# Local attention in pairs: paired score products, output tiles of their own, and one block-diagonal product for the meta keys

## The chip, the cores and the metric

The kernel runs on one core of a Trainium2 chip. The metric is the device time of one execution in microseconds (us). TensorE (PE in the profile, with PEld for its weight loads) does the matrix products and transposes, VectorE (DVE) and ScalarE (ACT) the elementwise work, GpSimd (POOL) some fills, and SyncE (SP) issues most of the transfers from memory.

## The reference, cut to what matters

Two transformer blocks follow each other. The change lies in the first one, whose sequence is 16 meta tokens and 512 tokens, with width 1024. Half of its mixer is a gated linear attention (GLA, 4 heads); the other half is a local attention with a sink, 8 query heads of 64 in 2 key groups of 4:

```python
qm, qr = q[:, :N_META], q[:, N_META:]
...
s_meta = jnp.einsum('bnqkgd,bjkd->bnkgqj', qb, km).astype(jnp.float32)
s_win = jnp.einsum('bnqkgd,bnjkd->bnkgqj', qb, kw).astype(jnp.float32)
...
p = sink_softmax(jnp.concatenate([s_meta, s_win], axis=-1),
                 sink[None, None, :, :, None, None]).astype(dtype)
orr = (jnp.einsum('bnkgqj,bjkd->bnqkgd', p[..., :N_META], vm)
       + jnp.einsum('bnkgqj,bnjkd->bnqkgd', p[..., N_META:], vw))
```

A block of 128 queries sees the 16 meta keys, the keys of its own block and those of the block before. Both halves, side by side, go through `w_out`; the result is added to the residual, normed, and enters a feed-forward part (`w_ff1`, squared ReLU, `w_ff2`).

## The kernel before, in words

The order of instructions on each engine is decided when the program is built, by a scheduler; the code gives the order of the steps and the pools their buffers. Products that need full precision are made of three: each operand is split into a high part (by ACT, `split`, L117) and a low part (by DVE, L118), and `mm3` issues low x high, high x low and high x high (L124 to L126).

`attention1` works through a list of steps, `PLAN`: q is a tile of the local queries (`w_sq`), r a tile of the GLA output gate (`w_gr`), p and g are two parts of a GLA chunk, s is one block of 128 queries of the local attention, o splits that block's output, t applies the gate. Tiles of q and r alternate between two PSUM banks (role mm of `PS_A`); scores have one bank (sw), transposes two (pt), and the attention output one (po).

One s step, `swa_block`, does for each of 8 heads one score product of 64 rows (L1632) and a masked reduction on DVE out of the score's bank (L1633). For each group of four heads follow the exponentials on ACT (L1637), the sums, and the scaling of p (L1645 on ACT, L1647 on DVE). Then for each group p is transposed (L1657), copied to SBUF (L1659) and multiplied with the values (L1660): one product for the block's own keys, one for the block before, and one of 16 rows with `mA` for the meta keys. The output in po is copied by DVE over the queries of the block (L1663), and split into `uh` and `ul` by the o step.

Behind the attention, `w_out` is computed in 8 tiles of 24 products; `w_out_ps` holds as many of them as mm has banks, made inside `attention1`. The residual is loaded (L251), `w_open` gives the first feed-forward group a ring of buffers for its weights (`w_load`, L483), and the group's products (`w_prod`, L499) compute x, z and w of a Strassen-like scheme with weights that are added, subtracted and split first (L536 to L555).

## Time and profile before

| what | us |
|---|---|
| median of 3 runs | 1934.77 (1934.54 to 1935.26) |
| the profiled execution | 1935.17 |
| its span in the profile | 1933.4 |
| PE busy | 1897.1 |
| DVE busy | 1482.6 |
| ACT busy | 864.4 |

The span runs from the first to the last instruction of the profiled execution, the rest of its time lies around it. Busy times are sums over the span; what a stage is bound by is read from windows and from what each engine waits for.

### The profile page before, as it was taken

The numbers are of one execution on the slowest core, as the hardware profiler recorded it, in microseconds if no ns is written. First come the engines' busy times: TensorE is split into PE (matmuls) and PEld (weight loads), VectorE is DVE, ScalarE is ACT, GpSimd is POOL, SyncE is SP. The second block draws the span as 40 slices with busy tenths as digits, with TensorE's granted clock in tenths as the row PEclk, the third lists the DMA queues.
The fourth block names the chain that finished last, engine by engine and source line by source line (L and its number), as shares of the span: only waits on it lengthen the run. The fifth ranks groups of instructions, "written<-read, shape, count | busy, mean of one in ns | idle before, by whom it ended". The sixth has DMA issues, their size and how long they took to land.

```text
span 1933.4 us, 27555 instructions
## 1 busy us (share of the span) xinstructions
PE 1897.1 (98%) x10808; PEld 1583.7 (82%) x10808; DVE 1482.6 (77%) x2507; ACT 864.4 (45%) x1406; POOL 9.4 (0%) x31
## 2 busy tenths in 40 slices
PE   8999999999999899999999999999999999999997
PEld 5775589898998699999887777777778888999997
DVE  6687599888888989888878646677758778877776
ACT  4334465443445545444455444344442245444444
POOL 0000000000000000000000000000000000000000
PEclk9999999999999999999999999999999999999999
DMA  5220045444534154546342232333348732333231
GB/s 198 67 61 12 28 176 177 141 145 152 162 111 142 57 175 142 183 137 202 109 142 88 87 119 69 104 96 99 99 145 308 270 116 78 118 112 108 89 99 55
DMA packets 74331, 240.46 MB, mean 124 GB/s; under 512 B 8997, under 2 KB 12214, under 8 KB 74202
## 3 DMA queue, kind: packets, MB, share of 16 engines
q1 hardware_dynamic: 57274, 189.75, 31.3%
q10 hardware_dynamic: 16928, 48.96, 8.0%
q8 instruction: 85, 1.39, 0.3%
q14 instruction: 44, 0.36, 0.1%
HBM read 225.74 MB, written 8.41 MB: 121 GB/s over the span
## 4 chain that ended last, share of the span: by engine, by line
PE 86%; DVE 9%; ACT 2%; DMA 2%; issue 1%; SPq 0%; DVEq 0%; ACTq 0%
PE x L499 12%; PE mm L132 10%; PE mm L131 10%; PE mm L130 10%; PE mm L124 6%; PE w L499 6%; PE mm L125 6%; PE mm L126 6%; PE z L499 3%; DVE wl L118 2%; PE po L1660 1%; PE sw L1632 1%; PE po L1186 1%; PE sc L1165 1%; PE sc L1047 1%
## 5 line engine op out<-in xcount | busy, mean ns | idle before, releaser
L117 ACT ACTIVATE wh<-raw 128x1024 fp32r<-128x1024 f32 (+1 forms) x371 | 386.3, 1044 | 430.6 <-PE mm L132 126.2
L118 DVE TENSOR_TENSOR wl<-raw,wh 128x1024 fp32r<-128x1024 f32 (+1 forms) x371 | 445.9, 1206 | 119.5 <-ACT wh L117 118.4
L132 PE MATMUL mm<-hh,wh 128*128 128x512 f32 (+1 forms) x640 | 244.6, 382 | 0.0
L131 PE MATMUL mm<-hl,wh 128*128 128x512 f32 (+1 forms) x640 | 244.0, 381 | 0.2 <-DVE hl L118 0.2
L130 PE MATMUL mm<-hh,wl 128*128 128x512 f32 (+1 forms) x640 | 241.7, 378 | 0.7 <-DVE res L694 0.7
L124 PE MATMUL mm<-uh,wl 128*128 128x512 f32 x560 | 225.8, 404 | 2.2 <-ACT uh L117 1.9
L126 PE MATMUL mm<-uh,wh 128*128 128x512 f32 x560 | 223.2, 399 | 0.0
L125 PE MATMUL mm<-ul,wh 128*128 128x512 f32 x560 | 222.4, 397 | 0.7 <-DVE ul L118 0.7
L131 PEld LDWEIGHTS mm<-hl,wh 128*128 128x128 f32 x640 | 120.2, 188 | 23.3 <-DVE hl L118 0.7
L130 PEld LDWEIGHTS mm<-hh,wl 128*128 128x128 f32 x640 | 120.1, 188 | 22.9 <-DVE res L694 0.9
L132 PEld LDWEIGHTS mm<-hh,wh 128*128 128x128 f32 x640 | 120.3, 188 | 21.6
L124 PEld LDWEIGHTS mm<-uh,wl 128*128 128x128 f32 x560 | 105.5, 189 | 33.5 <-issue 7.4
L126 PEld LDWEIGHTS mm<-uh,wh 128*128 128x128 f32 x560 | 105.4, 188 | 23.7 <-issue 2.3
L125 PEld LDWEIGHTS mm<-ul,wh 128*128 128x128 f32 x560 | 105.7, 189 | 23.3 <-issue 2.3
L499 PE MATMUL x<-uh,wl 128*128 128x256 f32 x416 | 115.2, 277 | 1.3 <-DVE wl L118 1.3
L499 PE MATMUL x<-vh,wl 128*128 128x256 f32 x416 | 116.1, 279 | 0.3 <-DVE wq__6174 L559 0.3
L499 PE MATMUL x<-vl,wh 128*128 128x256 f32 x416 | 115.4, 277 | 0.0
L499 PE MATMUL x<-vh,wh 128*128 128x256 f32 x416 | 115.1, 277 | 0.0
L499 PE MATMUL x<-ul,wh 128*128 128x256 f32 x416 | 115.0, 276 | 0.0
L499 PE MATMUL x<-uh,wh 128*128 128x256 f32 x416 | 114.9, 276 | 0.0
L356 DVE CUSTOM_DVE_ANT_0 adaw<-adaw,cb,c_vecs 128x1024 f32<-128x1024 f32 x72 | 91.4, 1277 | 11.1 <-DMA adaw<-in_w_ada 11.0
L622 DVE SCALAR_TENSOR_TENSOR res<-mm,gt,res 128x512 f32<-128x512 f32 x88 | 65.4, 746 | 23.0 <-PE mm L132 22.7
(970 smaller groups left out, 4222.2 us busy)
## 6 DMA issues: line engine op xcount, KB each, us to landing
adaw<-in_w_ada ACTq DMA_DIRECT2D x72, 512.0 KB
raw<-in_wgw SPq DMA_DIRECT2D x72, 512.0 KB
raw<-in_wdw SPq DMA_DIRECT2D x40, 512.0 KB
raw<-in_w_ffw SPq DMA_DIRECT2D x32, 512.0 KB
raw<-in_w_ffd SPq DMA_DIRECT2D x32, 512.0 KB
raw<-in_wgu SPq DMA_DIRECT2D x24, 512.0 KB
raw<-in_w_g SPq DMA_DIRECT2D x20, 512.0 KB
raw<-in_w_out SPq DMA_DIRECT2D x16, 512.0 KB
```

The costliest lines, as they stand in the source:

```text
L117: nc.scalar.activation(out=h, in_=src, func=AF.Copy)
L118: nc.vector.tensor_tensor(out=l, in0=src, in1=h.bitcast(F32), op=ALU.subtract)
L124: mm(ps, lhsT=wl[:, k], rhs=xh[:, k], start=(k == order[0]), stop=False)
L125: mm(ps, lhsT=wh[:, k], rhs=xl[:, k], start=False, stop=False)
L126: mm(ps, lhsT=wh[:, k], rhs=xh[:, k], start=False, stop=(k == order[-1]))
L130: mm(ps, lhsT=al, rhs=bh, start=(k == 0), stop=False)
L131: mm(ps, lhsT=ah, rhs=bl, start=False, stop=False)
L132: mm(ps, lhsT=ah, rhs=bh, start=False, stop=(k == last))
L356: ins = nc.vector.tensor_tensor_reduce(out=w, in0=w, in1=self.cb, scale=0.5, scalar=self.vec("b_ada_2", 72)[:, i:i + 1], op0=ALU.mult, op1 ...
L499: mm(o, lhsT=l[:, a, k], rhs=r(k), start=(first and a == 0 and k == 0 and j == 0), stop=(k == 3 and j == 2), skip_group_check=True)
L622: V.scalar_tensor_tensor(out=res[:, m], in0=ps, scalar=gt[:, m:m + 1], in1=res[:, m], op0=ALU.mult, op1=ALU.add)
L1047: mm(pk[:, :n], lhsT=k[:, kt, j * P:(j + 1) * P], rhs=q[:, kt, j * P:], start=(kt == 0), stop=(kt == 1))
```

## The change

Scores of the two groups, whose operands lie in rows 0 to 63 and 64 to 127, are computed in pairs into a tile of two PSUM banks, and the softmax of both groups follows behind the four pairs. That takes two banks for the scores; mm keeps one bank (0), and pt has banks 1 and 6 instead of 5 and 6. The transposes and value products of both groups are written part by part, with three buffers for pT. The meta keys' values stand in `vmb`, a block-diagonal 64 x 128 tile that is filled by a memset and two small transfers; the first group's p is transposed into rows 0 to 31 of a bank, the second group's is brought into rows 32 to 63 by products with the identity, and one product of 64 rows adds both groups' meta part to po. Three of four scalings are on ACT instead of two. po is split straight into `oh` and `ol`, tiles with a pool of their own, which is closed behind the w_out loop; the ring's pool is opened there, in the same memory. `w_out_tile` reads `oh` and `ol` first, then the GLA half of `uh` and `ul`, and one tile of w_out is made inside `attention1` instead of two. The steps o are gone.

```diff
-PS_A = dict(mm="01", ga="23", sw="4", pt="56", po="7")
+PS_A = dict(mm="0", ga="23", sw="4", pt="16", po="7")
...
-PLAN = "q0 q1 q3 p0 p1 q2 g0 s0 p2 g1 s2 s1 p3 r3 g2 g3 s3 r0 r2 r1 o0 o1 o2 o3 t01 t23"
...
+PTB = 3
+AO_SHIFT = 64
+RSQ = (0.3752467, -1.251589, 1.876343)
+PLAN = "q0 q1 q3 p0 p1 q2 g0 s0 p2 g1 s2 s1 p3 r3 g2 g3 s3 r0 r2 r1 t01 t23"
...
+        oe = ExitStack()
+        op = oe.enter_context(tc.tile_pool(name="ao", bufs=1, side="right"))
+        self.oh, self.ol = (op.tile([P, 4, T], F32R, name=n) for n in ("oh", "ol"))
+        self.shift(op, AO_SHIFT)
...
-        self.w_open(hp, 3)
...
-            ps = self.w_out_ps[m] if m < len(self.w_out_ps) else self.gemm("w_out", m, uh, ul)
+            ps = self.w_out_ps[m] if m < len(self.w_out_ps) else self.w_out_tile(m)
...
+        oe.close()
+        self.w_open(hpe.enter_context(tc.tile_pool(name="ring", bufs=1)), 3)
...
+        vmb = ap.tile([64, P], F32, name="vmb")
+        nc.gpsimd.memset(vmb, 0.0)
+        for g in range(2):
+            nc.sync.dma_start(out=vmb[32 * g:32 * g + NMETA, 64 * g:64 * g + 64], in_=mA[:, 384 + 64 * g:448 + 64 * g])
...
-        self.psum(**PS_A)
+        self.psum(pairs=True, **PS_A)
...
-        self.w_out_ps = [self.gemm("w_out", m, uh, ul, order=(4, 5, 6, 7, 0, 1, 2, 3)) for m in range(self.bufs["mm"])]
+        self.w_out_ps = [self.w_out_tile(m) for m in range(self.bufs["mm"])]
...
+    def w_out_tile(self, m):
+        wh, wl = self.wtile("w_out", m)
+        ps = self.mmps()
+        xs = [(4 + k, self.oh[:, k], self.ol[:, k]) for k in range(4)] + [(k, self.uh[:, k], self.ul[:, k]) for k in range(4)]
+        for j, (k, xh, xl) in enumerate(xs):
+            self.mm3k(ps, wh[:, k], wl[:, k], xh, xl, j)
+        return ps
...
-        pg = []
+        pg = [a2.tile([P, 4, NMETA + 2 * P], F32, name="p", tag="p") for g in range(2)]
+        for a in range(4):
+            pair = self.bank2("sw")
+            for g in range(2):
+                mm(pair[:, g, :W], lhsT=qT[64 * g:64 * g + 64, a, cs], rhs=keys[64 * g:64 * g + 64, :W], start=True, stop=True)
+            for g in range(2):
+                i = g * 4 + a
+                V.tensor_tensor_reduce(out=pg[g][:, a, :W], in0=pair[:, g, :W], in1=mk[:, :W], scale=1.0, scalar=sinks[:, i:i + 1], op0=ALU.add, op1=ALU.max, accum_out=mx[:, i:i + 1])
         for g in range(2):
-            p = a2.tile([P, 4, NMETA + 2 * P], F32, name="p", tag="p")
-            pg.append(p)
-            for a in range(4):
-                i = g * 4 + a
-                ps = self.bank("sw")
-                mm(ps[:, :W], lhsT=qT[64 * g:64 * g + 64, a, cs], rhs=keys[64 * g:64 * g + 64, :W], start=True, stop=True)
-                V.tensor_tensor_reduce(out=p[:, a, :W], in0=ps[:, :W], in1=mk[:, :W], scale=1.0, scalar=sinks[:, i:i + 1], op0=ALU.add, op1=ALU.max, accum_out=mx[:, i:i + 1])
+            p = pg[g]
             gs = slice(4 * g, 4 * g + 4)
             V.tensor_scalar(out=nmx[:, gs], in0=mx[:, gs], scalar1=-1.0, scalar2=None, op0=ALU.mult)
             for i in range(4 * g, 4 * g + 4):
@@ -1641,31 +1662,40 @@
             V.tensor_tensor(out=Z[:, gs], in0=Z[:, gs], in1=es, op=ALU.add)
             V.reciprocal(out=Z[:, gs], in_=Z[:, gs])
             for i in range(4 * g, 4 * g + 4):
-                if i % 2:
+                if i % 4:
                     act(out=p[:, i % 4, :W], in_=p[:, i % 4, :W], func=AF.Copy, scale=Z[:, i:i + 1])
                 else:
                     V.tensor_scalar(out=p[:, i % 4, :W], in0=p[:, i % 4, :W], scalar1=Z[:, i:i + 1], scalar2=None, op0=ALU.mult)
         po = self.bank("po")
-        for g in range(2):
-            parts = [(svt[:, n], P, W - P)]
-            if n > 0:
-                parts.append((svt[:, n - 1], P, NMETA))
-            parts.append((mA[:, 384:512], NMETA, 0))
-            for j, (v, nk, off) in enumerate(parts):
+        def pT(pt, n, func):
+            t = a2.tile([P, T], F32, name="pT", tag="pT", bufs=PTB)
+            func(out=t[:n], in_=pt[:n])
+            return t
+        copy = lambda out, in_: act(out=out, in_=in_, func=AF.Copy)
+        parts = [(svt[:, n], W - P, copy)]
+        if n > 0:
+            parts.append((svt[:, n - 1], NMETA, V.tensor_copy))
+        for j, (v, off, func) in enumerate(parts):
+            ts = []
+            for g in range(2):
                 pt = self.bank("pt")
                 for a in range(4):
-                    tr(pt[:nk, a * P:(a + 1) * P], pg[g][:, a, off:off + nk], ident)
-                pT = a2.tile([P, T], F32, name="pT", tag="pT", bufs=2)
-                (act if j != 1 else lambda out, in_, func: V.tensor_copy(out=out, in_=in_))(out=pT[:nk], in_=pt[:nk], func=AF.Copy)
-                mm(po[64 * g:64 * g + 64], lhsT=v[:, 64 * g:64 * g + 64], rhs=pT[:nk], start=(j == 0), stop=(j == len(parts) - 1))
-        o = qT[:, :, cs]
-        V.tensor_copy(out=o, in_=po.rearrange("p (a t) -> p a t", a=4))
-        return o
-    def swa_out(self, n, o):
-        cs = slice(n * P, (n + 1) * P)
-        self.split(self.uh[:, 4:8, cs], self.ul[:, 4:8, cs], o)
+                    tr(pt[:, a * P:(a + 1) * P], pg[g][:, a, off:off + P], ident)
+                ts.append(pT(pt, P, func))
+            for g in range(2):
+                mm(po[64 * g:64 * g + 64], lhsT=v[:, 64 * g:64 * g + 64], rhs=ts[g], start=(j == 0), stop=False, skip_group_check=True)
+        pt = self.bank("pt")
+        for a in range(4):
+            tr(pt[:32, a * P:(a + 1) * P], pg[0][:, a, 0:32], ident)
+        for a in range(4):
+            mm(pt[32:64, a * P:(a + 1) * P], lhsT=pg[1][:, a, 0:32], rhs=ident, start=True, stop=True)
+        t = pT(pt, 64, copy)
+        mm(po, lhsT=vmb, rhs=t[:64], start=False, stop=True, skip_group_check=True)
+        self.split(self.oh[:, :, cs], self.ol[:, :, cs], po.rearrange("p (a t) -> p a t", a=4))
```

On PE, scores and value products of the last blocks before: sw is a score, ga, po<-S and po<-gv are GLA products, pt transposes.

```order
L1632 MATMUL sw<-kW,qT 128x272
L1660 MATMUL po<-pT,svt 64x512
L1657 MATMUL pt<-ident,p 16x128 x4
L1660 MATMUL po<-pT,svt 64x512
L1576 MATMUL pt<-ident,E 128x128 x2
L126 MATMUL mm<-uh,wh 128x512
L1632 MATMUL sw<-kW,qT 128x272
L1660 MATMUL po<-pT,mA 64x512
L1487 MATMUL ga<-gv,kt 128x256 x2
L1632 MATMUL sw<-kW,qT 128x272
```

The same place now, up to the last pair:

```order
L1688 MATMUL po<-pT,svt 64x512 x2
L1693 MATMUL pt<-ident,p 32x128 x4
L1695 MATMUL pt<-ident,p 32x128 x4
L1595 MATMUL pt<-ident,E 128x128 x2
L1697 MATMUL po<-pT,vmb 128x512
L1506 MATMUL ga<-gv,kt 128x256 x2
L1649 MATMUL sw<-kW,qT 128x272 x2
L1587 MATMUL po<-S_797,E 128x256
L1590 MATMUL po<-gv,A 128x128 x2
L1587 MATMUL po<-S_797,E 128x256
L1590 MATMUL po<-gv,A 128x128 x2
L1649 MATMUL sw<-kW,qT 128x272 x2
```

Two scores stand next to each other where one stood between other work, and the meta part is one product.

On PE behind the last score before; mm<-uh or ul is a w_gr product up to the first transposes of gv, w_out behind them:

```order
L124 MATMUL mm<-uh,wl 128x512
L1660 MATMUL po<-pT,svt 64x512
L1657 MATMUL pt<-ident,p 16x128 x4
L125 MATMUL mm<-ul,wh 128x512
L1660 MATMUL po<-pT,svt 64x512
L126 MATMUL mm<-uh,wh 128x512
L124 MATMUL mm<-uh,wl 128x512
L1660 MATMUL po<-pT,mA 64x512
L125 MATMUL mm<-ul,wh 128x512
L126 MATMUL mm<-uh,wh 128x512
L1606 MATMUL pt<-ident,gv 128x128 x8
L124 MATMUL mm<-uh,wl 128x512 x2
```

And now, from the last pair's transposes to the first products of w_out:

```order
L1685 MATMUL pt<-ident,p 128x128 x8
L1688 MATMUL po<-pT,svt 64x512
L1685 MATMUL pt<-ident,p 128x128 x4
L1688 MATMUL po<-pT,svt 64x512 x2
L1693 MATMUL pt<-ident,p 32x128 x4
L1695 MATMUL pt<-ident,p 32x128 x4
L1625 MATMUL pt<-ident,gv 128x128 x4
L1697 MATMUL po<-pT,vmb 128x512
L1625 MATMUL pt<-ident,gv 128x128 x8
L132 MATMUL mm<-oh,wl 128x512
L133 MATMUL mm<-ol,wh 128x512
L134 MATMUL mm<-oh,wh 128x512
```

No w_gr product stands there any more, and w_out begins with oh.

On SP, the loads around w_out and the start of the feed-forward part before, with the semaphores that each waits for:

```order
L251 DMA res<-in_xT 128x1024
L111 DMA raw<-in_w_out 128x1024 [waits DMAHW0_49,DMAHW7_49,DVE_49,Activation_49]
L483 DMA raw<-in_w_ffw 128x1024 [waits DMAHW1_49]
L483 DMA raw<-in_w_ffw 128x1024 [waits DMAHW2_49]
L111 DMA raw<-in_w_out 128x1024 [waits DMAHW3_49,DVE_49]
L483 DMA raw<-in_w_ffw 128x1024 [waits DMAHW4_49]
L111 DMA raw<-in_w_out 128x1024 [waits DMAHW5_49,DVE_49]
```

And now:

```order
L258 DMA res<-in_xT 128x1024 x2
L113 DMA raw<-in_w_out 128x1024 [waits DMAHW2_49,DVE_49]
L113 DMA raw<-in_w_out 128x1024 [waits DMAHW4_49,DMAHW3_49,DVE_49]
L491 DMA raw<-in_w_ffw 128x1024 [waits DMAHW5_49,DVE_49]
L491 DMA raw<-in_w_ffw 128x1024 [waits DMAHW6_49,DMAHW2_49,DVE_49]
L491 DMA raw<-in_w_ffd 128x1024 [waits DMAHW7_49,DMAHW4_49,DVE_49]
L491 DMA raw<-in_w_ffw 128x1024 [waits DMAHW0_49,PE_49]
L491 DMA raw<-in_w_ffw 128x1024 [waits DMAHW1_49]
L491 DMA raw<-in_w_ffw 128x1024
```

The three loads of the ring (no wait but for their own queue before) now stand behind all of w_out's, and the first of them waits for PE.

## Rows read from the trace of the kernel before

**Rows 1.** The page, parts 1 (busy time) and 4 (the chain that ended last).

```profile
PE 1897.1 (98%) x10808; PEld 1583.7 (82%) x10808; DVE 1482.6 (77%) x2507; ACT 864.4 (45%) x1406; POOL 9.4 (0%) x31
...
PE 86%; DVE 9%; ACT 2%; DMA 2%; issue 1%; SPq 0%; DVEq 0%; ACTq 0%
```

**Rows 2.** Windows: window, its length, busy by engine, PE clock, DMA share, GB/s.

```profile
100.00:215.00 115.00, 114.94 (x541) 75.18 (x540) 88.87 (x288) 51.11 (x151) 1.05 (x2) 1.00 0.12 35
```

**Rows 3.** Timeline of PE: start, duration, line, operands, idle before; scores and neighbours.

```profile
121.73 0.51 PE L1632 MATMUL sw<-kT,qT 64*128 64x144 f32 x2
...
205.98 0.72 PE L1632 MATMUL sw<-kW,qT 64*128 64x272 f32 x2
206.63 1.07 PE L1660 MATMUL po<-pT,mA 16*64 16x512 f32 x2
```

**Rows 4.** Timeline of PE in block 2: two score products of 384 columns.

```profile
1261.01 0.92 PE L1165 MATMUL sc<-g 64*128 64x384 f32 x4
```

**Rows 5.** Timeline of PE: two GLA products; two value products (two records each).

```profile
213.09 0.61 PE L1571 MATMUL po<-gv,A 128*128 128x128 f32 x4
...
216.47 1.93 PE L1660 MATMUL po<-pT,svt 128*64 128x512 f32 x4
```

**Rows 6.** Timeline of PE from the last score to w_out.

```profile
214.51 0.72 PE L1632 MATMUL sw<-kW,qT 64*128 64x272 f32 x2
...
221.00 1.09 PE L1657 MATMUL pt<-ident,p 128*128 128x128 f32 x8
...
230.32 0.73 PE L124 MATMUL mm<-uh,wl 128*128 128x512 f32 x2 [1.93 <-ACT uh L117]
231.73 0.55 PE L125 MATMUL mm<-ul,wh 128*128 128x512 f32 x1 [0.68 <-DVE ul L118]
```

**Rows 7.** Timeline of DVE: the last score's reduction, a w_gr tile's read.

```profile
215.27 0.50 DVE L1633 CUSTOM_DVE_ANT_0 p<-sw,c_mask_w,c_vecs 128x272 f32<-128x272 f32 x1 [2.71 <-PE sw L1632]
...
227.56 0.69 DVE L1425 TENSOR_TENSOR rr<-mm,R 128x512 f32<-128x512 f32 x1
```

**Rows 8.** Timeline of ACT: an exponential and its accumulator's read, two scalings.

```profile
218.13 0.51 ACT L1637 ACTIVATE p<-p,nmx 128x272 f32<-128x272 f32 x1
218.54 0.19 ACT L1637 ACTIVATION_READ_ACCUMULATOR p<-p,nmx 128x1 f32 x1
...
219.52 0.92 ACT L1645 ACTIVATE p<-p,Z 128x272 f32<-128x272 f32 x2
```

**Rows 9.** Windows, columns as in rows 2: the half-clock stretch.

```profile
232.00:235.40 3.40, 3.40 (x11) 2.64 (x11) 3.40 (x6) 1.26 (x2) 0.00 (x0) 0.50 0.00 0
```

**Rows 10.** Timeline of PE: end of w_out, first feed-forward group.

```profile
277.36 0.39 PE L125 MATMUL mm<-ul,wh 128*128 128x512 f32 x1
277.58 0.40 PE L126 MATMUL mm<-uh,wh 128*128 128x512 f32 x1
277.82 0.28 PE L499 MATMUL x<-vh,wl 128*128 128x256 f32 x1
...
288.44 0.39 PE L499 MATMUL x<-uh,wl 128*128 128x256 f32 x1 [1.31 <-DVE wl L118]
```

**Rows 11.** Timeline of SP: issues of 512 KB weight loads.

```profile
240.19 2.77 SPq L483 DMA_DIRECT2D raw<-in_w_ffw  x2
...
394.02 0.33 SPq L425 DMA_DIRECT2D raw<-in_wgu  x1
```

**Rows 12.** Timeline of DVE: feed-forward weight passes; the first read of the load issued at 394.02.

```profile
256.23 2.36 DVE L118 TENSOR_TENSOR wl<-raw,wh 128x1024 fp32r<-128x1024 f32 x2
...
274.93 1.21 DVE L118 TENSOR_TENSOR wl<-raw,wh 128x1024 fp32r<-128x1024 f32 x1
...
398.52 0.29 DVE L427 TENSOR_SCALAR pa<-raw,mods 128x128 f32<-128x128 f32 x1 [1.15 <-DMA raw<-in_wgu]
```

**Rows 13.** Windows of 20 us, columns as in rows 2.

```profile
260.00:280.00 20.00, 20.00 (x99) 16.79 (x98) 19.85 (x29) 12.67 (x18) 0.00 (x0) 1.00 0.26 80
...
300.00:320.00 20.00, 19.76 (x133) 17.75 (x132) 19.48 (x25) 10.99 (x16) 0.00 (x0) 1.00 0.39 125
```

More of the change, by code (lines that the diff above doesn't have):

```diff
@@ L28 @@
 NPRE = 2
-RSQ = (0.3752467, -1.251589, 1.876343)
-PS_A = dict(mm="01", ga="23", sw="4", pt="56", po="7")
+PS_A = dict(mm="0", ga="23", sw="4", pt="16", po="7")
 MM5, AT2, PG1 = "01234", "56", "7"
@@ L1220, in attention1 @@
         wn = self.vec("norm_mix_w")
-        mh = ap.tile([P, KT, NMETA], F32R, name="mh")
-        ml = ap.tile([P, KT, NMETA], F32R, name="ml")
         acc = {}
@@ L1226, in attention1 @@
         x = bp.tile([P, KT, T], F32, name="x")
+        mh = bp.tile([P, KT, NMETA], F32R, name="mh")
+        ml = bp.tile([P, KT, NMETA], F32R, name="ml")
         mt = bp.tile([P, KT, NMETA], F32, name="mt")
@@ L1326, in attention1 @@
         self.dump("kT", kT)
+        vmb = ap.tile([64, P], F32, name="vmb")
+        nc.gpsimd.memset(vmb, 0.0)
+        for g in range(2):
+            nc.sync.dma_start(out=vmb[32 * g:32 * g + NMETA, 64 * g:64 * g + 64], in_=mA[:, 384 + 64 * g:448 + 64 * g])
         raw = bp.tile([P, KT, 16], F32, name="lr_f")
         nc.sync.dma_start(out=raw, in_=I["w_lr"])
-        lh = ap.tile([P, KT, 16], F32R, name="lh")
-        ll = ap.tile([P, KT, 16], F32R, name="ll")
+        lh = bp.tile([P, KT, 16], F32R, name="lh")
+        ll = bp.tile([P, KT, 16], F32R, name="ll")
         self.split(lh, ll, raw)
@@ L1395, in attention1 @@
         sr = ap.tile([P, NB, T], F32, name="sr")
-        self.psum(**PS_A)
+        self.psum(pairs=True, **PS_A)
         p1 = lambda c: self.gla_part1(c, a2, dmat, gh, gl, gkT, gqT, lvl)
-        sw = lambda c: self.swa_block(c, ap, a2, kT, kW, qT, svt, mA, mask_w, sinks)
+        sw = lambda c: self.swa_block(c, ap, a2, kT, kW, qT, svt, vmb, mask_w, sinks)
         self.qd = [ap.tile([P, 2, 2, 64], F32, name=f"qd{i}") for i in range(NQD)]
@@ L1427, in rgate @@
             V.scalar_tensor_tensor(out=sr[:, i], in0=th, scalar=1.0, in1=rr, op0=ALU.add, op1=ALU.mult)
-        e, so, S = {}, {}, [S]
+        e, S = {}, [S]
         for step in PLAN.split():
@@ L1442, in attention1 @@
             elif f == "s":
-                so[c] = sw(c)
-            elif f == "o":
-                self.swa_out(c, so[c])
+                sw(c)
             elif f == "t":
                 gate(*divmod(c, 10))
-        self.w_out_ps = [self.gemm("w_out", m, uh, ul, order=(4, 5, 6, 7, 0, 1, 2, 3)) for m in range(self.bufs["mm"])]
+        self.w_out_ps = [self.w_out_tile(m) for m in range(self.bufs["mm"])]
         self.dump("wo_h", self.uh)
@@ L1609, in gla_gate, with swa_block @@
             self.split(self.uh[:, 0:4, cs], self.ul[:, 0:4, cs], og)
-    def swa_block(self, n, ap, a2, kT, kW, qT, svt, mA, mask_w, sinks):
+    def swa_block(self, n, ap, a2, kT, kW, qT, svt, vmb, mask_w, sinks):
         nc = self.nc
```

## The prediction

> **What bounds the kernel now.** I read the page first: TensorE is busy for 98% of the span, and the chain that ended last runs over PE for 86% and over DVE for 9% of it [rows 1]. The reader should see that an average like this hides stages with other limits, so I asked for windows around the changed part. In 100 to 215 us, where most of the attention lies, PE has 114.94 us of work in 115, at full clock (1.00, the 2.4 GHz level), and DVE 88.87 [rows 2]: PE work that goes away there is time, as long as no new wait takes its place. Then I followed PE to its gaps. One stands behind the last score (214.51), ahead of w_out's first product: 1.93 us for ACT's split of the attention output, then 0.68 for DVE's [rows 6]. From there to 277.58 w_out's stream runs on, and the first FF group's first product follows it at 277.82 with no gap; PE next waits for a weight split (1.31, DVE) at 288.44 [rows 10]. Last I asked for windows across that point: DVE is busy for 19.85 of 20 us from 260 to 280, and for 19.48 from 300 to 320 [rows 13]. That stretch belongs to DVE as much as to PE.
>
> **The change part by part.**
>
> *Score pairs.* 32 products of 64 rows become 16 pairs, of which 14 stand side by side in the new order. A 272-column product holds PE for 206.63 - 205.98 = 0.65 us, one of 144 columns, which shows 0.51, with the same overlap of 0.07 for 0.44 [rows 3]. Block 2 has the nearest row for a pair: its two 384-column products of 64 rows in two halves of a bank pair are over in 0.92 together [rows 4], and one of 272 columns alone takes 0.72, so a pair costs about one product. Saved: 10 x 0.65 + 4 x 0.44 = 8.3 us; nothing, if pairs don't overlap.
>
> *Meta products.* 8 of 16 rows become 4 block-diagonal ones. They are as long as any 512-column product (1.93 / 2 = 0.97, [rows 5]), so 4 x 1.0 = 4.0 saved, 3.0 of it in the first three blocks. 16 of the 32 meta transposes become fp32 products: 0.61 / 2 = 0.30 each [rows 5] for 1.09 / 8 = 0.14 [rows 6], so +2.6, 1.9 of it in the first three blocks.
>
> *Column halves.* The value products of the two groups write different halves of one bank, but only 3 of 7 couples stand side by side. No row shows such halves overlapping: 0 to 3 x 0.93 = 2.8 saved; the row has four records in 1.93 with no overlap [rows 5], so I take 0. The Trainium skill, "TensorE: Matmul & The Clock Gate", Part 3 (measured speedup), has three column tiles run 2.38 times as fast as one after the other; by that an estimate for the three couples is the 2.8, and the sum would be 2.8 lower. No row of this case shows it.
>
> *One bank for mm.* In before, w_sq and w_gr tiles alternate between two banks. Now each next tile waits until DVE has read the one ahead: about 0.1 to start and 0.69 [rows 7], so 0.8 for each of 7 hand-overs, 5.6 if nothing covers it, 0 if other PE rows do. *One pair tile.* The next pair waits for two reductions of 0.50 [rows 7] where there was one: up to 12 x 0.5 = 6.0 more. DVE is 77% busy here [rows 2], so its reads do not come at once. The Trainium skill, "TensorEngine Tiling (Array Packing)", sections PSUM Bottleneck and Gotcha 1, says that packing speeds up TensorE and not the emptying of PSUM, which then may bound. The rows agree: a pair of 0.7 us leaves DVE 1.0 us of reductions. By that rule nothing of the 8.3 would be left.
>
> *Sum to the last score.* -8.3 - 3.0 + 1.9. 15 w_gr products that stood behind the last score as filler (five of them are in the piece of the old order shown) are now ahead of it; at a slot of 0.23 (277.36 to 277.82 for two, [rows 10]) that is +3.5. Together -5.9; with 4.9 of waits given back I take **-1.0**. Bounds: -8.7 (column halves too, no wait) and +5.7 (all of 5.6 and 6.0).
>
> *From the last score to w_out.* Before 230.32 - 214.51 = 15.8: 6.5 to the transposes of the last group at 221.00, 9.3 behind [rows 6]. Before, one group's softmax was left; now that of both, for both need the last pair. In the new ACT order four exponentials, the sink's, three of the other group and three scalings stand ahead of the first transposes: 1.9 to the end of the second reduction, 0.3 for nmx, 7 x 0.41 + 0.1 (218.13 to 218.54), 3 x 0.46 [rows 8], 0.7 for DVE's part and hand-overs: 7.3. Behind them: one exponential, the sink's, a copy and three scalings (2.5), eight transposes (0.9), a copy (0.8), three value products (2.9), meta transposes and products (1.5), copy (0.8), the block-diagonal product (1.0), ACT's first half of the output split (0.8): 11.0 in a row, since each needs the one ahead and no w_gr product is left to fill. 18.3 for 15.8: **+2.5**. The copy of the output to qT (0.69 on DVE) is gone from this chain and counted so. Bounds 0 and +5.
>
> *w_out.* Before: 277.82 - 230.32 = 47.5. 192 products at 0.23 are 44.2; the rest is the 0.68 wait, gate transposes, and 3.4 us at clock 0.50 from 232.0 on [rows 9], the 1.2 GHz level, granted behind PE's two idle stretches of 1.93 and 0.68; that cost 1.7. After: 44.2 + 0.5 for gate transposes, so -2.8; but PE idles longer in the new tail, so I keep a half-clock stretch of the same size, there: +1.7. **-1.1**, bounds -2.8 and +2.
>
> *Start of the first FF group.* This is the largest term. In before the ring's weights were issued at 240.19 [rows 11], and split by 274.93, before w_out ended. Now ring memory is memory that oh and ol held, and SP's row for the first load waits for PE's last product that reads them. That is in w_out's last tile, with 12 uh products behind it: 12 x 0.23 = 2.7 us. Behind the waiting row on SP stand the other loads of the group, in order. A load of this size issued at 394.02, with another one just ahead, was first read at 398.52: 4.5 [rows 11, 12]. ACT's half of the split adds 1.05 and DVE's 1.13: 4.5 + 2.2 - 2.7 = **4.0** during which PE has nothing. Then DVE: 8 passes of the FF group (the first pair at 256.23, 2.36 for two, the last at 274.93, [rows 12]) lay ahead of 277.8, where DVE had room; 8 x 1.13 = 9.0 us of work now come after the load lands, 4.5 - 2.7 = 1.8 behind w_out's end, into the stretch in which DVE was already 97 to 99% busy [rows 13]. So the group comes 1.8 + 9.0 = **10.8** later; the 4.0 lies within it. Bounds: 4.0 (DVE makes it up) and 14 (three loads share the rate and land later).
>
> *Clock at that start.* 4 us of idle PE: 0 to +1.7 by the stretch of rows 9; **+0.5**.
>
> *The rest costs nothing.* The o steps go away (4 copies of 0.69 on DVE in blocks not at the end, hidden beside PE). Three scalings of four on ACT: ACT is busy 51.11 of 115 [rows 2]; price without cover 0.46 each, counted in the tail. The small vmb loads stand far ahead of their use.
>
> Sum: -1.0 + 2.5 - 1.1 + 10.8 + 0.5 = +11.7. On the profiled execution's own time, 1935.2 (its span of 1933.4 and 1.8 around it), this is 1946.9; the median of the runs is 0.4 lower: **1946.5**.
>
> **The rivals.**
> - *DVE makes it up.* The FF group's late passes spread over the next stages, and only the 4.0 us wait for the load counts: +4.9, 1939.7. For it: PE, not DVE, waits in few places behind 290. Against: the windows of DVE at 97% or more [rows 13]. 0.17.
> - *Half clock holds.* PE idles some 6 us in the tail, and the 1.2 GHz level lasts through the chain's products and into w_out: 4 more, 1950.5. For it: rows 9 after shorter idling. 0.14.
> - *Pairs do not overlap:* the 8.3 stay, 1954.8. Against: rows 4. 0.07.
> - *Faster: DVE is never waited for.* One mechanism: DVE's hand-overs in PSUM and its displaced passes are covered, PE's slots count in full and the clock stays up: -8.7 + 2.5 - 2.8 + 4.0 = -5.0, 1929.8. Place: the mm bank before 215 and the FF start. It decides if what DVE adds at both places together is under 5.0; I count 4.9 + 6.8. For it: rows 2 show PE as the only full engine up to 215. Against: rows 13. 0.05.
> - *The change does not do what it says,* or gains and losses meet: pairs give back all, the load is hidden by uh products more than counted, within 3.9 us (0.2%, about what a measurement of this kernel can tell from no change): 0.05.
>
> **How the numbers follow.** The forecast has 0.52, the rivals 0.17, 0.14, 0.07, 0.05 and 0.05. Its own range, from the terms' nearer bounds, is 1942 to 1951. The range 1939 to 1954 takes in the made-up case and the half clock, and leaves out the two fast cases and most of the no-overlap case, some 0.17. Faster by over 0.2%: 0.05; within: 0.05; slower: 0.90.
>
> **What would show it.** Right: two records of the new score line starting together; PE idle of 4 to 6 us between the last score pair and w_out's first product on oh, named for ACT or DVE; SP's first ring load issued about 2.7 us before w_out's last product; a PE gap of about 4 us before the first x product, for DVE's or ACT's split and a DMA behind it; more PE waits for DVE until some 330. Wrong: ring loads issued in w_out's middle; the FF group's second wait no longer than before; or a last score near 208, by which the slots came off in full.

## The result, and the profile after

The changed kernel takes 1954.28 us (median of 4 runs, 1953.42 to 1956.75) against 1934.65 for the kernel before on the same chip: a ratio of 1.0099 with a 95% interval of 1.0086 to 1.0111, about 19.6 us or 1.0% slower. The sign was forecast; the size lies 7.8 us above the forecast of 1946.5, and 0.3 above the top of the range. The execution whose profile follows is the longest of the four (1956.75): from 365.68, where the third feed-forward group starts, to its end it takes as long as the kernel before (1589.2 and 1588.9 us), so distances read from it ahead of that point may be up to 2.5 us longer than in a run at the median.

The page of the profile after, its span, busy times (part 1) and chain (part 4), answers to [rows 1]:

```profile
span 1954.9 us, 27558 instructions
...
PE 1898.8 (97%) x10816; PEld 1588.4 (81%) x10816; DVE 1479.0 (76%) x2493; ACT 866.5 (44%) x1412; POOL 9.6 (0%) x32
...
PE 87%; DVE 7%; ACT 3%; DMA 1%; issue 1%; DVEq 0%; ACTq 0%; SPq 0%
```

This page hides what happened. PE's busy time is 1.7 us longer than before, though the change removes products. A PE at half clock shows as busy (7.08 of 7.10 us at a clock of 0.54 in one window below), so the windows have to be read with their clock, the last number but two. Windows of the kernel after:

```profile
100.00:215.00 115.00, 108.14 (x529) 72.89 (x527) 83.98 (x264) 49.37 (x138) 1.05 (x2) 0.97 0.13 39
...
170.60:178.00 7.40, 6.25 (x24) 4.89 (x25) 7.02 (x26) 5.68 (x21) 0.00 (x0) 0.60 0.00 0
225.70:236.00 10.30, 9.54 (x24) 3.68 (x24) 2.10 (x6) 4.11 (x11) 0.00 (x0) 0.62 0.00 0
291.90:299.00 7.10, 7.08 (x34) 6.93 (x35) 6.61 (x12) 1.77 (x2) 0.00 (x0) 0.54 0.37 103
303.70:310.00 6.30, 6.25 (x34) 5.50 (x35) 6.30 (x9) 2.35 (x4) 0.00 (x0) 0.73 0.45 119
325.60:330.00 4.40, 4.36 (x24) 4.39 (x25) 4.40 (x5) 3.10 (x4) 0.00 (x0) 0.61 0.07 5
```

In [rows 2] PE was idle for 0.06 us of 115, now for 6.9. And where [rows 9] had one stretch at the 1.2 GHz level, there are now five stretches with a mean clock of 0.54 to 0.73. Length times the missing share is an estimate of what each took: 3.0, 3.9, 3.3, 1.7 and 1.7, together 13.6 us, against 3.4 x 0.5 = 1.7 before. It is an estimate since the windows also hold a little idle time.

Each of the five follows a wait of PE. The timeline of PE after (start, duration, line, operands, and in brackets the idle time before and what ended it) at the longest waits:

```profile
170.61 0.73 PE L1649 MATMUL sw<-kT,qT 64*128 64x272 f32 x4 [1.72 <-DVE mx L1652]
...
204.20 1.07 PE L1688 MATMUL po<-pT,svt 128*64 128x512 f32 x2 [1.24 <-ACT pT L1676]
...
208.25 1.93 PE L1688 MATMUL po<-pT,svt 128*64 128x512 f32 x4
...
219.88 0.73 PE L1649 MATMUL sw<-kW,qT 64*128 64x272 f32 x4
225.77 1.52 PE L1685 MATMUL pt<-ident,p 128*128 128x128 f32 x4 [5.16 <-DVE p L1668]
...
240.41 0.48 PE L132 MATMUL mm<-oh,wl 128*128 128x512 f32 x1
...
250.90 0.50 PE L132 MATMUL mm<-oh,wl 128*128 128x512 f32 x1 [1.60 <-DVE res L275]
...
287.17 0.40 PE L134 MATMUL mm<-uh,wh 128*128 128x512 f32 x1
291.92 0.55 PE L507 MATMUL x<-vh,wl 128*128 128x256 f32 x1 [4.35 <-issue]
...
303.75 0.39 PE L507 MATMUL w<-uh,wl 128*128 128x256 f32 x1 [2.06 <-DVE wl L120]
...
325.64 0.48 PE L507 MATMUL w<-uh,wl 128*128 128x256 f32 x1 [2.23 <-DVE wl L120]
```

The last score stands at 219.88 for 214.51 in [rows 6], w_out's first product at 240.41 for 230.32, the first x product at 291.92 for 277.82 in [rows 10]. SP, ACT and DVE show what the 4.35 us ahead of x, named "issue", waited for. SP issued the ring's three loads at 284.85, 2.5 us ahead of w_out's end at 287.4, behind its wait for PE. ACT split the first of them at 288.57 with no wait, so it had landed by then, at most 3.7 us after its issue. DVE's half came at 290.60, 1.0 us behind ACT's, since other passes stood ahead of it in DVE's queue; when it is done, x starts:

```profile
284.85 1.28 SPq L491 DMA_DIRECT2D raw<-in_w_ffw  x3
```

```profile
288.57 1.04 ACT L119 ACTIVATE wh<-raw 128x1024 fp32r<-128x1024 f32 x1
...
291.55 1.06 ACT L119 ACTIVATE wh<-raw 128x1024 fp32r<-128x1024 f32 x1 [0.29 <-DMA raw<-in_w_ffw]
```

```profile
289.07 1.22 DVE L120 TENSOR_TENSOR ul<-hh,uh 128x1024 fp32r<-128x1024 f32 x1
...
290.60 1.22 DVE L120 TENSOR_TENSOR wl<-raw,wh 128x1024 fp32r<-128x1024 f32 x1
```

The work that DVE no longer does under w_out shows in two windows from w_out's first product to its end, the first of the kernel after, the second of the kernel before:

```profile
240.40:287.40 47.00, 45.10 (x199) 36.27 (x197) 29.51 (x48) 22.19 (x32) 0.00 (x0) 1.00 0.41 132
```

```profile
230.30:277.80 47.50, 46.80 (x200) 38.02 (x201) 39.93 (x60) 26.63 (x38) 0.00 (x0) 0.96 0.48 169
```

DVE did 39.93 us there and now does 29.51, 10.4 us less. It had fifteen passes of 1024 columns there and now has seven: eight fewer, the number that the prediction counted, at 9.0 us. The rest of the 10.4 is smaller passes.

**The account nearly closes.** PE's waits over 0.1 us between the last product of the common part (93.17 before, 93.46 after) and the first x product of the third feed-forward group add up to 5.2 us before (1.93, 0.68, 0.99, 1.31, 0.24) and 23.6 after (7.1 ahead of the last score; 5.2, 0.7, 0.2 and 0.3 in the tail, the stretch from there to w_out's first products; 1.6 in w_out; then 4.35, 2.06 and 2.23): +18.4. Half clock is +11.9. That x product starts at 344.49 before and at 365.68 after, 20.9 us later counted from the common product. By this estimate 18.4 + 11.9 - 20.9 = 9.4 us of PE work did come off; the prediction's slots are 8.3 + 4.0 - 2.6 = 9.7. How near the two are may be partly chance, for the half clock's share is not exact: filling the wait of 5.16 (busy_tail, below) brings 2.3 us at w_out's start where this working has 3.9.

### The profile page after: what moved, and what is told of

It reads as the page before. It is cut to its first block, busy times and chain, and to the rows that moved or that the text cites. A ratio compares the mean times of both kernels' runs of the same rounds, so it can differ in the third digit from the quotient of the medians.

```text
span 1954.9 us, 27558 instructions
## 1 busy us (share of the span) xinstructions
PE 1898.8 (97%) x10816; PEld 1588.4 (81%) x10816; DVE 1479.0 (76%) x2493; ACT 866.5 (44%) x1412; POOL 9.6 (0%) x32
## 4 chain that ended last, share of the span: by engine, by line
PE 87%; DVE 7%; ACT 3%; DMA 1%; issue 1%; DVEq 0%; ACTq 0%; SPq 0%
PE x L507 13%; PE mm L134 11%; PE mm L133 11%; PE mm L132 11%; PE w L507 7%; PE mm L126 6%; PE mm L128 6%; PE mm L127 6%; PE z L507 3%; DVE wl L120 1%; PE po L1194 1%; PE sc L1173 1%; PE sc L1055 1%; PE pn L1063 1%; PE pr L128 1%
## 5 line engine op out<-in xcount | busy, mean ns | idle before, releaser
L126 PE MATMUL mm<-uh,wl 128*128 128x512 f32 x496 | 201.3, 406 | 2.0 <-DVE qT L1500 1.2
L128 PE MATMUL mm<-uh,wh 128*128 128x512 f32 x496 | 198.3, 400 | 0.0
L127 PE MATMUL mm<-ul,wh 128*128 128x512 f32 x496 | 197.4, 398 | 0.0
L126 PEld LDWEIGHTS mm<-uh,wl 128*128 128x128 f32 x496 | 93.5, 189 | 31.0 <-issue 6.6
L128 PEld LDWEIGHTS mm<-uh,wh 128*128 128x128 f32 x496 | 93.6, 189 | 20.4 <-issue 1.4
L127 PEld LDWEIGHTS mm<-ul,wh 128*128 128x128 f32 x496 | 93.7, 189 | 18.5 <-issue 1.0
L364 DVE CUSTOM_DVE_ANT_0 adaw<-adaw,cb,c_vecs 128x1024 f32<-128x1024 f32 x72 | 91.4, 1278 | 12.6 <-DMA adaw<-in_w_ada 12.4
L507 PEld LDWEIGHTS x<-vh,wl 128*128 128x128 f32 x416 | 79.2, 190 | 6.8 <-issue 4.8
```

The costliest lines, as they stand in the source:

```text
L126: mm(ps, lhsT=wl[:, k], rhs=xh[:, k], start=(k == order[0]), stop=False)
L127: mm(ps, lhsT=wh[:, k], rhs=xl[:, k], start=False, stop=False)
L128: mm(ps, lhsT=wh[:, k], rhs=xh[:, k], start=False, stop=(k == order[-1]))
L364: ins = nc.vector.tensor_tensor_reduce(out=w, in0=w, in1=self.cb, scale=0.5, scalar=self.vec("b_ada_2", 72)[:, i:i + 1], op0=ALU.mult, op1 ...
L507: mm(o, lhsT=l[:, a, k], rhs=r(k), start=(first and a == 0 and k == 0 and j == 0), stop=(k == 3 and j == 2), skip_group_check=True)
```

## The experiments

Runs of one kernel also differ by 1 to 3 us in stages that no edit touches (busy_tail's trace loses 1.8 us between 556 and 689). So for each run the table has, beside the ratio to the kernel before on the same chip, the starts of three products in its PE timeline: the last common one near 93 (A), the first x product, and the first x product of the third group, at 344.49 in the kernel before (the mark); from there on the order of instructions is the same in all. "Late" is the mark less A, less the same in the kernel before (251.32).

| kernel | median us | ratio (95%) | A | first x | mark | x late | mark late |
|---|---|---|---|---|---|---|---|
| before | 1934.65 | 1 | 93.17 | 277.82 | 344.49 | 0 | 0 |
| after | 1954.28 | 1.0099 (1.0086 to 1.0111) | 93.46 | 291.92 | 365.68 | 13.8 | 20.9 |
| raw_early | 1948.62 | 1.0070 (1.0055 to 1.0085) | 92.62 | 286.44 | 357.69 | 9.2 | 13.8 |
| last_by_group | 1953.66 | 1.0095 (1.0080 to 1.0110) | 93.57 | 289.42 | 365.64 | 11.2 | 20.8 |
| all_by_group | 1950.42 | 1.0078 (1.0063 to 1.0093) | 92.61 | 286.14 | 360.43 | 8.9 | 16.5 |
| mm_two_banks | 1958.50 | 1.0126 (1.0109 to 1.0143) | 93.15 | 290.44 | 364.06 | 12.6 | 19.6 |
| ring_early_ada_late | 1950.20 | 1.0078 (1.0063 to 1.0094) | 93.00 | 284.98 | 360.42 | 7.3 | 16.1 |
| ring_early_by_group | 1944.64 | 1.0047 (1.0033 to 1.0061) | 93.18 | 279.35 | 353.04 | 1.5 | 8.5 |
| busy_tail | 1956.07 | 1.0110 (1.0096 to 1.0124) | 93.68 | 289.82 | 364.71 | 11.5 | 19.7 |
| before_meta | 1936.50 | 1.0003 (0.9995 to 1.0012) | 93.63 | 279.85 | 346.00 | 1.6 | 1.1 |
| before_ao | 1945.02 | 1.0046 (1.0032 to 1.0060) | 92.46 | 279.38 | 353.24 | 2.3 | 9.5 |
| before_pairs | 1940.09 | 1.0019 (1.0009 to 1.0028) | 93.17 | 282.86 | 349.35 | 5.0 | 4.9 |
| before_banks | 1942.10 | 1.0030 (1.0018 to 1.0042) | 93.80 | 286.85 | 352.69 | 8.4 | 7.6 |
| before_busy_gap | 1935.88 | 0.9996 (0.9987 to 1.0005) | 92.00 | 275.47 | 344.27 | -1.2 | 1.0 |

**raw_early.** The ring's raw and sum buffers get memory of their own, its wh and wl buffers keep that of oh and ol:

```diff
         hp = hpe.enter_context(tc.tile_pool(name="hid", bufs=1))
+        self.w_open(hp, 3)
...
         oe.close()
-        self.w_open(hpe.enter_context(tc.tile_pool(name="ring", bufs=1)), 3)
+        self.hw = hpe.enter_context(tc.tile_pool(name="ring", bufs=1))
...
-        return (self.hp if own else self.wp).tile(
+        return ((self.hp if tag == "raw" else self.hw) if own else self.wp).tile(
```

Expected: 

> The changed kernel, with the ring's raw, sum and difference buffers in memory of their own, opened ahead of w_out; only the ring's wh and wl buffers still take the memory of oh and ol. My theory (the late loads push nine us of DVE passes behind w_out): the loads are issued in w_out's middle, the gap of 4.35 us ahead of the first x product falls under 1 us, the second wait shrinks, and 8 us come back: 1946, 1943.5 to 1949. Rival (only the idle gap itself counts): 4.4 come back, 1950. Rival (DVE bounds that stretch whatever the loads do): 1953 to 1955.

Measured: the loads are issued from 244.76 on, and PE's timeline shows the gap ahead of x gone, but two waits of 2.3 left. Its window behind x follows:

```profile
286.44 0.39 PE L508 MATMUL x<-vh,wl 128*128 128x256 f32 x1 [0.34 <-DVE wl L120]
...
295.97 0.42 PE L508 MATMUL w<-ul,wh 128*128 128x256 f32 x1 [2.26 <-DVE ul L120]
...
318.39 0.36 PE L508 MATMUL w<-uh,wl 128*128 128x256 f32 x1 [2.27 <-DVE wl L120]
```

```profile
286.00:293.00 7.00, 6.66 (x57) 6.44 (x57) 6.92 (x12) 4.61 (x7) 0.00 (x0) 1.00 0.13 53
```

At the mark 7.1 of the 20.9 us are back, near the 8 expected, and 5.7 of the median. The median, 1948.6, is inside my range but nearer the first rival's 1950. And the second wait did not shrink, as I had said it would: 2.06 became 2.26. From x to the mark PE's waits over 0.3 us fall only from 8.6 to 5.9; the rest of what came back is the half clock behind x, which is at 1.00 here and was at 0.54. So the rival that only the gap counts is right about the waits, and what it lacks is the half clock behind the gap. That the splits which still wait for oh's memory keep the rest is argued, not shown.

**ring_early_ada_late.** All split buffers of the ring are opened early; oh's and ol's memory goes to the ada weights (pool on the other side, started behind w_out) and to the two sum buffers:

```diff
+        self.w_open(hp, 3)
...
-        self.w_open(hpe.enter_context(tc.tile_pool(name="ring", bufs=1)), 3)
+        self.hs = hpe.enter_context(tc.tile_pool(name="ring", bufs=1))
+        self.ada_start(self.ue.enter_context(tc.tile_pool(name="ada", bufs=1, side="right")))
...
-        S = self.hp.tile([P, 2 * T], F32, name="wS", tag="wS", bufs=1)
+        S = self.hs.tile([P, 2 * T], F32, name="wS", tag="wS", bufs=1)
```

Expected: 

> The changed kernel, with the ring's raw, wh and wl buffers opened ahead of w_out as before, and oh's and ol's memory given instead to the ada weights and to two sum buffers. My theory (the FF start's 11.5 us, gap and displaced passes, come from the late ring): x starts right behind w_out, the waits for wl behind it go, and 10 us come back: 1944.5, 1942 to 1947.5. Rival (the ada loads, now late, take the ring's place): 1950 to 1955.

Measured: x starts with no wait, 6.5 us earlier than after, and then PE stands still for the split of the sum. The sum and its split on DVE follow, with one of the ada passes between:

```profile
284.98 0.28 PE L506 MATMUL x<-vh,wl 128*128 128x256 f32 x1
...
297.61 0.58 PE L506 MATMUL w<-uh,wl 128*128 128x256 f32 x1 [4.90 <-DVE wl L120]
```

```profile
283.57 1.22 DVE L543 TENSOR_TENSOR wS<-raw 128x1024 f32<-128x1024 f32 x1
...
293.85 1.28 DVE L363 CUSTOM_DVE_ANT_0 adaw<-adaw,cb,c_vecs 128x1024 f32<-128x1024 f32 x1
...
296.34 1.22 DVE L120 TENSOR_TENSOR wl<-wS,wh 128x1024 fp32r<-128x1024 f32 x1
```

4.8 come back at the mark, 4.1 of the median: the rival's number. The late sum and ada passes (each 1.2 to 1.3 on DVE) now stand where the ring's splits stood. So at the start of this group PE waits for DVE's queue with other late passes too: behind w_out's end 8.8 us are lost (16.1 - 7.3), for 11.6 in the changed kernel.

**last_by_group and all_by_group.** The four scores of a group, two at a time in the two banks, then that group's softmax; in the last block (n == 3) or in all:

```diff
-        for a in range(4):
-            pair = self.bank2("sw")
...
+        alone = n == 3
+        def score(heads):
+            pair = self.bank2("sw")
+            for j, (g, a) in enumerate(heads):
+                mm(pair[:, j, :W], lhsT=qT[64 * g:64 * g + 64, a, cs], rhs=keys[64 * g:64 * g + 64, :W], start=True, stop=True)
...
         for g in range(2):
+            if alone:
+                for a in (0, 2):
+                    score([(g, a), (g, a + 1)])
```

Expected of the first: 

> The changed kernel, with the scores of the last block alone in the old order (four of one group, softmax, four of the other), two at a time in the two banks, so without overlap. My theory (the tail grew since both softmaxes wait for the last pair): the transposes start 2 us earlier behind the last score, the half clock is shorter, and 2.6 us of slots come back: 1952.5, 1950.5 to 1954.5. Rival (the tail is long because the clock falls, not because of the order): tail as long as before, 1955 to 1957.

Measured: two products of the same rows take 1.18 for a pair's 0.73; the wait in the tail is 2.85 for 5.16, and w_out starts 16.7 us behind the last scores for 20.5:

```profile
220.59 1.18 PE L1650 MATMUL sw<-kW,qT 64*128 64x272 f32 x4
...
237.24 0.48 PE L132 MATMUL mm<-oh,wl 128*128 128x512 f32 x1
```

So the tail is long by the order of the softmax, as expected. But the median is only 0.6 lower, within the spread of the runs, and of the 2.6 us that x gained, the mark has 0.1 left: the start of the feed-forward group took them.

Expected of the second: 

> The changed kernel, with all scores in the old order of groups, two at a time in the two banks, so that none overlap. My theory (the pairs' 8.3 us of slots were given back by waits for DVE): within 3 us of the changed kernel, 1951.5 to 1957. Rival (the slots are real gain and the loss came from elsewhere): 8.3 longer less 2 in the tail, about 1960.5.

Measured: 4.4 us earlier at the mark than the changed kernel, below my range. Of the waits of 1.72, 1.24, 0.85 and 0.62 that the kernel after has between 120 and 215 only the last is left (0.61), and all windows from 100 to 215 show full clock. Giving up the overlap, and with it the wait of both softmaxes for the last pair, was worth more here than the pairs' slots.

**mm_two_banks.**

```diff
-PS_A = dict(mm="0", ga="23", sw="4", pt="16", po="7")
+PS_A = dict(mm="01", ga="23", sw="4", pt="6", po="7")
```

Expected: 

> The changed kernel, with two banks for mm again and one for the transposes. My theory (hand-overs of the one mm bank cost most of the 6 us that PE waits ahead of the last score, and with them the half clock): 4 us come back, 1950, 1948 to 1952. Rival (one bank for transposes costs as much, since two copies must pass it in each part): 1954 to 1959.

Measured: the median is 4.2 above the changed kernel's, the rival's number, and its runs spread from 1953.8 to 1962.0. The trace is of the fastest of them, so its mark, 1.3 earlier, does not stand for the median. No gain: the waits for the one mm bank, 1.6 us in the changed kernel, are gone, and in their place stand waits at the one transpose bank:

```profile
194.83 1.52 PE L1685 MATMUL pt<-ident,p 128*128 128x128 f32 x4 [2.23 <-DVE p L1668]
197.96 1.97 PE L1688 MATMUL po<-pT,svt 128*64 128x512 f32 x2 [1.61 <-ACT pT L1676]
```

**ring_early_by_group.** Both edits together. Expected: 

> The kernel of ring_early_ada_late, with all scores in the old order of groups too. My theory (the two losses lie in different places and add): 10 and 3.9 us back, 1940.5, 1938 to 1943.5, still above before by the rest of the tail. Rival (DVE takes the gain of the one away when the other is mended): about 1944, no better than ring_early_ada_late.

Measured: 12.4 us earlier at the mark than the changed kernel, 9.6 in the median, while the two alone gave 4.8 and 4.4. So the two do not merely add: together they give more at the mark than the sum of both. The time is still above my range of 1938 to 1943.5 and at the rival's 1944, though not for its reason, since the rival had no gain over ring_early_ada_late (1950.2). It is the best of the changed kernels, and still 0.47% slower than before.

**busy_tail.** Six products behind the last pair, read by nobody:

```diff
+        if n == 3:
+            idle = self.bank("ga")
+            for i in range(6):
+                mm(idle[:4, :W], lhsT=nmx[:, 0:4], rhs=mk[:, :W], start=True, stop=True)
         po = self.bank("po")
```

Expected: 

> The changed kernel with 6 extra score-sized products, whose result nobody reads, on PE between the last pair and the first transposes, where it idles for 5.2 us; all else is the same, in the same order. My theory (the half clock in the tail follows from that idle stretch, and costs 4 us of products at half speed): the clock stays at 1.00, and w_out starts 4 us earlier though PE has more to do: 1950.3, 1949 to 1952. Rival (the tail is a chain of ACT and DVE, the clock matters little): 1953.5 to 1955.

Measured: the idle stretch is filled (1.11 and 1.14 us are left of 5.16), the clock stays at 1.00, and w_out starts at 238.26, 18.2 us behind the last pair for 20.5. Its timeline, then its windows of the tail and behind x:

```profile
220.03 0.73 PE L1649 MATMUL sw<-kW,qT 64*128 64x272 f32 x4
221.88 2.91 PE L1672 MATMUL ga<-c_mask_w,nmx 128*4 128x272 f32 x12 [1.11 <-DVE es L1660]
225.93 1.37 PE L1689 MATMUL pt<-ident,p 128*128 128x128 f32 x4 [1.14 <-DVE p L1668]
...
238.26 0.48 PE L132 MATMUL mm<-oh,wl 128*128 128x512 f32 x1
```

```profile
225.90:236.00 10.10, 8.79 (x40) 4.11 (x40) 2.08 (x5) 4.32 (x12) 0.00 (x0) 1.00 0.00 0
289.80:297.00 7.20, 7.18 (x33) 7.08 (x34) 6.71 (x14) 1.59 (x2) 0.00 (x0) 0.50 0.37 103
```

That idling brings the half clock in the tail is shown, and its price there is 2.3, not 4. At the mark 1.2 are left, and the whole run, at 1956.1, is not faster: it lies above my range and the rival's.

**before_meta.** The block-diagonal meta product alone, in the kernel before (its memset, two loads, transposes and product as in the changed kernel). Expected: 

> The kernel before with the block-diagonal meta product alone. My theory (that part is a gain by itself): 4 products of 1.0 less, 16 transposes that become products of 0.25 for 0.14, so 2.2 faster, 1932.6, 1931 to 1934. Rival (the last block's one meta product waits for both groups and lengthens the tail): 1935 to 1937.

Measured: no change, 1.0003. PE now waits for the single score bank between the last scores (0.71, 0.90, 0.60) and 1.41 for p, while the slots come off elsewhere: neither a gain nor a loss. My gain of 2.2 did not come, and the time is in the rival's range.

**before_ao.** The output tiles and the late ring alone, in the kernel before:

```diff
-            self.split(self.uh[:, 4:8, cs], self.ul[:, 4:8, cs], o)
+            self.split(self.oh[:, :, cs], self.ol[:, :, cs], o)
...
-        self.w_open(hp, 3)
...
+        oe.close()
+        self.w_open(hpe.enter_context(tc.tile_pool(name="ring", bufs=1)), 3)
```

Expected: 

> The kernel before with the output tiles oh and ol, w_out reading them first, and the ring opened behind w_out in their memory; attention, banks and steps are those of before. My theory (the late ring costs its 10.8 us by itself): the first ring load waits for PE, a gap of about 4 us stands ahead of the first x product, and the stage behind it loses as much again: 1946, 1944 to 1948.5. Rival (it hurts only because DVE is already late in the changed kernel): under 5 us lost, 1936 to 1940.

Measured: 1945.0, inside my range; the same gap as in the changed kernel, to the hundredth, and the same next wait:

```profile
279.38 0.55 PE L505 MATMUL x<-vh,wl 128*128 128x256 f32 x1 [4.35 <-issue]
...
291.35 0.39 PE L505 MATMUL w<-uh,wl 128*128 128x256 f32 x1 [2.06 <-DVE wl L118]
```

x is 2.3 late behind a gap of 4.35, so w_out ended 2.1 earlier than before; from there to the mark it loses 9.5 + 2.1 = 11.5 us. The late ring costs this alone, with the old attention.

**before_pairs and before_banks.** The changed kernel's banks in the kernel before, with the score pairs and both softmaxes behind them, or with the scores by group:

```diff
-PS_A = dict(mm="01", ga="23", sw="4", pt="56", po="7")
+PS_A = dict(mm="0", ga="23", sw="4", pt="16", po="7")
...
-        self.psum(**PS_A)
+        self.psum(pairs=True, **PS_A)
```

Expected of the first: 

> The kernel before with the changed kernel's banks and its score pairs with both softmaxes behind the last pair; value products, meta products, steps and ring are those of before. My theory (pairing loses what its slots save, by waits for DVE and in the tail): 5 to 10 us slower, 1942, 1938.5 to 1946. Rival (pairs are a gain, the loss comes from the other edits of the attention): 1930 to 1935.

Expected of the second: 

> The same with the scores in the old order of groups, two at a time in the two banks, each group's softmax behind its own four: what is left is the plan of banks, with one bank for mm. My theory (waits for the one mm bank are mostly covered): 0 to 3 us slower, 1936.5, 1934.5 to 1938. Rival (the one mm bank is the main loss): as slow as before_pairs.

Measured: pairs cost 4.9 us at the mark, the banks without pairs 7.6. The pairs lose, as I held. The bank plan without pairs loses about as much, outside my range for before_banks (1934.5 to 1938), so its rival is nearer, though no run tells the one mm bank from the rest of the plan. By the marks the overlap is worth some 2.7 there, where in the new attention it costs 4.4. But the medians differ by 2.0 and the runs of before_banks spread over 7.2 us, so it is not shown that pairs gain anything in the old attention. What these runs show is that they do not cost there what they cost in the new one.

**before_busy_gap.** Three such products in the gap of [rows 6]:

```diff
+            if i == 1:
+                idle = self.bank("ga")
+                for _ in range(3):
+                    mm(idle[:4, :272], lhsT=rr[:, 0:4], rhs=mask_w[:, :272], start=True, stop=True)
```

Expected: 

> The kernel before with 3 extra products, whose result nobody reads, on PE between the first gate transposes and w_out's first product, where it idles for 1.93 us. My theory (the half clock from 232.0 to 235.4 follows from that idle stretch): the clock stays at 1.00, w_out ends 1.5 us earlier, 1933.3, 1932.5 to 1934.5, a gain at the edge of what can be measured. Rival (the clock falls anyway, or the extra products are in the way): 1934.8 or more.

Measured: no change (0.9996), the rival's number, though the clock did stay up where I had said. The wait ahead of w_out falls from 1.93 to 0.46, the stretch of [rows 9] is at 1.00, and x starts 1.2 us earlier; but a stretch behind x, at 1.00 in the kernel before, is now at 0.67:

```profile
232.00:235.40 3.40, 3.40 (x19) 2.83 (x18) 3.40 (x6) 1.54 (x3) 0.00 (x0) 1.00 0.00 0
...
282.00:287.00 5.00, 5.00 (x30) 4.84 (x29) 3.67 (x10) 2.19 (x3) 0.00 (x0) 0.67 0.33 105
```

The second window in the kernel before, and the two waits ahead of it here:

```profile
282.00:287.00 5.00, 4.12 (x35) 4.05 (x35) 5.00 (x11) 3.67 (x6) 0.00 (x0) 1.00 0.21 36
```

```profile
279.13 0.39 PE L499 MATMUL z<-vh,wl 128*128 128x256 f32 x1 [0.67 <-DVE res L269]
...
281.20 1.27 PE L218 MATMUL at<-ones,ssq 128*128 128x1 f32 x8 [0.99 <-DVE ssq L210]
```

In this trace the half clock has moved to the next place where PE waits. The first of the two waits is new: in the kernel before only the 0.99 stands there. The gain of 1.2 at x is a loss of 1.0 at the mark, within what runs differ by. No version beats the kernel before.

## Why the prediction was right or wrong

*Sum to the last score: wrong.* Forecast -1.0, measured +5.1 (219.88 - 93.46 against 214.51 - 93.17). The slots were right: a pair takes 0.73 and the next product starts 0.66 behind it. The step that failed is "with 4.9 of waits given back": the waits are 7.1 (0.69 at 97.06 to 0.37 at 212.45), and behind those at 170 to 173 stand 3.0 us of half clock that I had not counted at all. -5.9 + 7.1 + 3.0 is +4.2; 0.9 stays open. Their kind was off too: DVE's reads of the one mm bank cost 1.6 (0.69, 0.23, 0.24 and 0.45), of a ceiling of 5.6, and mm_two_banks gains nothing that could be measured; the large ones are the pair tile (1.72) and ACT's copies of pT (1.24, 0.36, 0.37).

*Column halves: right.* Two value products of the two groups, side by side, take 1.93 after as in [rows 5]; 0 of the 2.8. The Trainium skill's figure in "TensorE: Matmul & The Clock Gate", Part 3, does not show for these two halves of 64 columns; the measurement decides. The prediction's 2.8 was full overlap; the Trainium skill's 2.38 for three tiles, carried over to two halves, would be an estimate of 2.1.

*Last score to w_out: the sum right but for the clock, its parts not.* Forecast 18.3, measured 20.5. With the clock kept up (busy_tail) it is 18.2, so the term is short by the half clock in it, which I had put in the next term at 1.7. That 18.2 meets 18.3 is luck: up to the first transposes it is 5.9 in both traces (219.88 to 225.77, 220.03 to 225.93) where I had 7.3, and behind them 12.3 in busy_tail where I had 11.0. The items that I listed for the 11.0 also add up to 11.2.

*w_out: -1.1, measured -0.5* (47.0 for 47.5). The 1.7 of half clock that I kept here did not come, for w_out runs at 1.00. A 1.60 us wait for the residual sum, not foreseen, takes its place: DVE waits 4.72 us for the res load, which SP issues at 244.10, behind the longer tail.

*Start of the feed-forward group: right in sum, half of it for another reason.* Forecast 10.8 + 0.5, measured 20.9 - 9.3 = 11.6 behind w_out's end, and 11.5 in before_ao; the gap 4.35 for 4.0, with a load that is faster than I took (at most 3.7 us for 4.5) and a wait in DVE's queue (1.0) that I did not have; and the eight DVE passes moved. But the waits add only 8.6 - 2.5 = 6.1. The other part is the half clock behind them, for which I had 0.5: an estimate of 3.3 + 1.7 + 1.7 = 6.7. Together that is 12.8, 1.2 above the 11.6, so the estimate is somewhat high. That the two meet my sum is partly luck.

*The rival of the half clock* had the mechanism that the forecast lacked, with 4 us in one place; it is 11.9 more over five places. The rival that pairs don't overlap, though its time is the nearest (1954.8), is wrong. DVE did not make up its late passes.

*What stays open.* Late at the mark, alone in the old kernel: tiles and ring 9.5, pairs and banks 4.9, meta 1.1; together 15.4 of 20.9. The other 5.5 may be the parts' effect on each other, edits that no run had alone (scalings, parts in turns, the direct split), and the long execution from which the 20.9 is read; which of them is open. In the order of instructions, w_gr products behind the last score number 15 before, 8 in before_pairs and 0 after; that the missing filler is the reason is argued, not shown.

## What to carry to other kernels

A buffer that takes another's memory waits for that memory's last reader: ask which queue its load stands in, and which passes of a full engine move behind it, since here 4.35 us of visible gap stood for 11.5. Where TensorE is the bound, count each new wait twice: once for itself and once for the half clock that may follow. And a saved slot is worth something only if the reader of its result isn't waited for; test a packing in the schedule in which it will stand.

## What the runs showed that I had not expected

Filling an idle stretch can move the half clock instead of removing it, as one trace here shows. Filling the 1.93 us ahead of w_out kept the clock at 1.00 there (0.50 before), and a stretch 50 us later, which had run at 1.00 behind waits of 0.99, came to 0.67 behind waits of 0.67 and 0.99. Filling 5.16 us in the changed kernel gave 2.3 us at w_out's start and 1.2 at the mark.

Two score products of the same 64 rows, side by side, take 1.18 us from the first's start to the second's end, where one alone shows 0.72. A pair of different rows takes 0.73, so the overlap itself saves 0.45, less than the 0.65 for which a pair was priced.
